# Squared-ReLU feed-forwards of a two-layer trunk as seven block products for eight, with operand sums passed through DRAM

## The chip, the cores and the metric

The kernel runs on one core of one Trainium2 chip, so there is no traffic between cores. The metric is the device time of one execution in microseconds (us), the median over runs. The profile is that of one execution: spans, durations and the granted TensorE clock are from it.

## The reference

All numbers are float32, with 1024 tokens of 1024 features. There are two layers: the first mixes tokens with a short gated convolution, the second with latent attention of eight heads. Each mixer is followed by a feed-forward of 4096 hidden features, and each of these four sub-layers by a normalisation over the residual:

```python
def _sq_relu_mlp(x, w1, w2):
    return jnp.square(jax.nn.relu(x @ w1)) @ w2
...
    for i in range(DEPTH):
...
        x = _layer_norm(ALPHA * x + y, ln_mix_g[i], ln_mix_b[i])
        x = _layer_norm(ALPHA * x + _sq_relu_mlp(x, ff_w1[i], ff_w2[i]), ln_ff_g[i], ln_ff_b[i])
    return x
```

Here `y` is the mixer's output, `w1` is 1024x4096, `w2` 4096x1024.

## The kernel before

**Products in three matmuls.** TensorE computes in a rounded type (float32r). Each float32 operand is therefore cut by `split` into a high part, a cast on ScalarE (L78), and a low part, source minus high part on VectorE (L79). `mm3` (L94) adds three matmuls into one PSUM bank: high by high (L96), high by low (L97), low by high (L98). `piece` (L85) loads a weight block of 128x1024 in two halves on the queue of SyncE (L90, tile `raw`, two buffers) and splits it into a `w` tile (five buffers). Activations with both their parts lie in `act` tiles of 128x1024 (34 buffers), products in eight PSUM banks of 128x512 (`pB`).

**A feed-forward.** `ffn` (L224) walks the hidden features in 32 blocks of 128, `m`. Tokens lie in two halves of 512, and `st.xt[half]` holds the transposed input as eight pairs of parts, one for each 128 features. For a block and a half, `ff1` sums eight products (24 matmuls), and `ffn_act` (L216) applies Relu on ScalarE (L218) and squares on VectorE (L219), then splits the result. Four blocks make a chunk. For a chunk, `token_out` (L118) sums four products (12 matmuls) for each of eight token tiles and two column halves and adds the bank to the residual tile `xrs[t]` on VectorE (L128 in the first chunk, which also multiplies the residual by ALPHA, L130 in later ones). The up-projection of the next chunk is written between the down-projections of two chunks.

**Around it.** The last chunk of every sub-layer but the final one is `last_chunk` (L199): after a tile's last addition, `ln_z` (L153) normalises it in place (two statistics L142, an aggregate L144, a root on ScalarE L146, four small operations L147 to L150, the scaling L155). Transposes (`ln_T`, L157) of the first four tiles are written behind tiles 4 to 7; those of the last four come in the next sub-layer, where `st.pump` takes them from the list. The gain and bias of the transposed input are applied on ScalarE (L162); those of the residual are applied by GpSimd in the first part of the next feed-forward (`tail_affine`, L211, through L180 and L181, 32 operations in place in `xrs`). After the second feed-forward, the final loop adds the last chunk, normalises, applies gain and bias, and stores the output from L668.

The program is one list in the order in which it is written. Each engine takes its own instructions of it in order and waits where an operand or a buffer isn't there yet. The same holds for the queues of SyncE, ScalarE and GpSimd that issue transfers.

## Time and profile before

| | |
|---|---|
| time, median of 3 runs | 2269.17 us (2267.36 to 2269.52) |
| span of the profiled execution, first to last instruction | 2269.7 us |
| TensorE matmul / weight load, share of the span | 98% / 82% |
| VectorE, ScalarE, GpSimd | 50%, 29%, 8% |
| transfers | 123.61 MB, mean 54 GB/s |

The profiled execution's own time is its span; nothing else lies around it. The median of the runs is 0.5 us below it. Shares are those of busy time over the whole span, which has stages of different kinds: the two feed-forwards run from about 375 to 1090 us and from about 1550 to 2260 us.

### The profile page before, as it was taken

Reading aid. Unit: us, or ns where it says so; the run is one execution under the profiler, and the core shown is the slowest. Engines: PE = TensorE matmul, PEld = TensorE weight load, DVE = VectorE, ACT = ScalarE, POOL = GpSimd, SP = SyncE. Lnnn points to the kernel's source line nnn. Section 1 sums busy time; section 2 is a strip of 40 time slices with the busy share of each in tenths; the row PEclk is TensorE's granted clock in tenths of the full one; section 3 lists DMA queues with packets and bytes.
Section 4 is the critical chain, followed back from the end, with each engine's and each line's share of the span. In section 5 each row is a group of like instructions: output and inputs, shape, how many; then the busy total and the mean of one; then the engine's idle time right before and its main releaser. Section 6 shows DMA issues by size and latency. Waiting matters only on the chain.

```text
span 2269.7 us, 25964 instructions
## 1 busy us (share of the span) xinstructions
PE 2217.9 (98%) x10360; PEld 1852.0 (82%) x10360; DVE 1135.9 (50%) x2002; ACT 650.9 (29%) x1239; POOL 184.9 (8%) x215
## 2 busy tenths in 40 slices
PE   8999998999999999999999999998999999999998
PEld 7888887788888888888888888786888888888886
DVE  5433459533433433436467778879343333333337
ACT  4111214321321311312456565333221221221222
POOL 0000007100000000000000002317000000000004
PEclk9999999999999999999999999998999999999999
DMA  5211211110210210212200011211111110110111
GB/s 188 100 38 44 68 48 47 56 56 19 75 53 23 75 47 28 74 44 78 76 6 21 15 39 47 93 47 56 47 65 36 48 63 30 56 56 28 65 47 74
DMA packets 64248, 123.61 MB, mean 54 GB/s; under 512 B 7280, under 2 KB 10352, under 8 KB 64128
## 3 DMA queue, kind: packets, MB, share of 16 engines
q1 hardware_dynamic: 56592, 99.64, 13.4%
q0 software_dynamic: 5088, 17.87, 2.3%
q10 hardware_dynamic: 2448, 4.46, 0.6%
q8 instruction: 81, 1.33, 0.2%
q14 instruction: 39, 0.32, 0.0%
HBM read 113.55 MB, written 8.39 MB: 54 GB/s over the span
## 4 chain that ended last, share of the span: by engine, by line
PE 88%; DVE 7%; DMA 2%; ACT 1%; issue 1%; SPq 0%; DVEq 0%; POOL 0%; ACTq 0%
PE pB L97 28%; PE pB L96 28%; PE pB L98 28%; DVE act L79 2%; DVE w L79 1%; DVE tmp L219 1%; PE pB L558 1%; DMA raw<-in_w_o 1%; ACT tmp L429 1%; PE pA L526 0%; PE pA L527 0%; PE pA L528 0%; PE pA L529 0%; PE pA L530 0%; DVE stat L142 0%
## 5 line engine op out<-in xcount | busy, mean ns | idle before, releaser
L96 PE MATMUL pB<-act,w 128*128 128x512 f32 x1608 | 631.1, 393 | 15.5 <-ACT act L78 9.7
L97 PE MATMUL pB<-act,w 128*128 128x512 f32 x1608 | 629.9, 392 | 0.3 <-DVE act L79 0.2
L98 PE MATMUL pB<-act,w 128*128 128x512 f32 x1608 | 628.8, 391 | 0.0
L96 PE MATMUL pB<-w,act 128*128 128x512 f32 (+1 forms) x1504 | 563.2, 375 | 1.8 <-DVE act L128 0.7
L97 PE MATMUL pB<-w,act 128*128 128x512 f32 (+1 forms) x1504 | 562.2, 374 | 1.7 <-DVE w L79 1.7
L98 PE MATMUL pB<-w,act 128*128 128x512 f32 (+1 forms) x1504 | 561.0, 373 | 0.0
L78 ACT CAST w<-raw 128x512 fp32r<-128x512 f32 x366 | 213.6, 613 | 793.0 <-PE pB L98 647.3
L96 PEld LDWEIGHTS pB<-act,w 128*128 128x128 f32 x1608 | 304.3, 189 | 79.4 <-ACT act L78 10.9
L97 PEld LDWEIGHTS pB<-act,w 128*128 128x128 f32 x1608 | 304.1, 189 | 64.3 <-DVE act L79 1.8
L98 PEld LDWEIGHTS pB<-act,w 128*128 128x128 f32 x1608 | 304.0, 189 | 63.7
L130 DVE TENSOR_TENSOR act<-act,pB 128x512 f32<-128x512 f32 x256 | 175.4, 685 | 348.7 <-PE pB L98 347.2
L96 PEld LDWEIGHTS pB<-w,act 128*128 128x128 f32 x1504 | 283.0, 188 | 56.5 <-ACT w L78 3.8
L97 PEld LDWEIGHTS pB<-w,act 128*128 128x128 f32 x1504 | 283.1, 188 | 54.2 <-DVE w L79 4.1
L98 PEld LDWEIGHTS pB<-w,act 128*128 128x128 f32 x1504 | 283.1, 188 | 49.7
L79 DVE TENSOR_TENSOR w<-raw,w 128x512 fp32r<-128x512 f32 x366 | 246.9, 695 | 151.1 <-ACT w L78 150.1
L219 DVE TENSOR_TENSOR tmp<-tmp 128x512 f32<-128x512 f32 x128 | 109.2, 853 | 266.3 <-ACT tmp L218 266.2
L79 DVE TENSOR_TENSOR act<-tmp,act 128x512 fp32r<-128x512 f32 x204 | 160.1, 795 | 58.0 <-ACT act L78 58.0
L78 ACT CAST act<-tmp 128x512 fp32r<-128x512 f32 x204 | 123.6, 621 | 148.4 <-DVE tmp L219 77.3
L218 ACT ACTIVATE tmp<-pB 128x512 f32<-128x512 f32 x128 | 76.3, 596 | 284.4 <-PE pB L98 283.8
L128 DVE SCALAR_TENSOR_TENSOR act<-act,pB 128x512 f32<-128x512 f32 x64 | 43.8, 686 | 92.2 <-PE pB L98 92.0
L667 POOL TENSOR_TENSOR act<-act,row 128x512 f32<-128x512 f32 x13 | 17.2, 1320 | 651.5 <-DVE act L666 651.0
L180 POOL TENSOR_TENSOR act<-act,row 128x512 f32<-128x512 f32 x40 | 61.9, 1565 | 92.2 <-DVE stat L142 69.4
(112 smaller groups left out, 1252.9 us busy)
## 6 DMA issues: line engine op xcount, KB each, us to landing
raw<-in_w_f SPq DMA_DIRECT2D x256, 256.0 KB, 2.7
raw<-in_w_sci SPq DMA_DIRECT2D x42, 256.0 KB, 2.7
act<-in_xT ACTq DMA_DIRECT2D x16, 256.0 KB, 4.4
act<-in_x POOLq DMA_DIRECT2D x8, 512.0 KB, 9.4
raw<-in_w_sco SPq DMA_DIRECT2D x16, 256.0 KB, 2.7
row<-in_grow POOLq DMA_DIRECT2D x16, 256.0 KB, 3.7
spill<-act POOLq DMA_DIRECT2D x8, 512.0 KB, 2.9
raw<-in_w_o SPq DMA_DIRECT2D x16, 256.0 KB, 2.7
```

The source lines that it names most:

```text
L78: nc.scalar.copy(hi, src)
L79: nc.vector.tensor_tensor(lo, src, hi.bitcast(F32), op=ALU.subtract)
L96: nc.tensor.matmul(ps, lh, rh, start=first, stop=False)
L97: nc.tensor.matmul(ps, lh, rl, start=False, stop=False)
L98: nc.tensor.matmul(ps, ll, rh, start=False, stop=last)
L128: nc.vector.scalar_tensor_tensor(xr[:, s], xr[:, s], ALPHA, ps, op0=ALU.mult, op1=ALU.add)
L130: nc.vector.tensor_tensor(xr[:, s], xr[:, s], ps, op=ALU.add)
L180: engs[d].tensor_tensor(xr[:, s], xr[:, s], gr[d], op=ALU.mult)
L218: nc.scalar.activation(r, ps, AF.Relu)
L219: nc.vector.tensor_tensor(r, r, r, op=ALU.mult)
L429: nc.scalar.copy(b[j * 32:(j + 1) * 32], ps[k * 32:(k + 1) * 32])
L558: nc.tensor.transpose(ps[:, j * P:(j + 1) * P], p[:, (q4 + j) * P:(q4 + j + 1) * P], ident)
```

## The change

Both projections of both feed-forwards are cut in 2x2 blocks and computed with seven products of blocks and their sums (Winograd's form of Strassen's algorithm) in place of eight products.

**Up-projection.** The hidden blocks are taken in 16 pairs `p` and `p + 16`, the features in two halves of four, the tokens in two halves. A product `k` of a pair is four `mm3`, 12 matmuls, in one bank. `load` brings the two weight blocks of a pair; `sums` makes four sums of weight blocks on GpSimd (L255 to L258); `operand` splits the weight operand of one product into an `fp` tile (eight buffers), and `ahead` keeps six operands ready. The inputs of products 4 to 7 are differences of the transposed input, made once in `combine` (L346, for `k == 7` on GpSimd, else on VectorE). `begin` and `rest` add the banks into the four output blocks on VectorE (`add`, L293), apply Relu and Square on ScalarE, make four sums, and store seven operands for the down-projection in DRAM (`hs`) through SyncE. The first four pairs (`LEAD`) run products 1 and 2, then 3, then 6, 7, 5 and 4; transposes of the last four token tiles lie between them, and the four `combine` calls between the products 3.

**Down-projection.** It runs product by product, in the order 1, 2, 5, 6, 3, 7, 4, each over all 16 pairs in four banks, 192 matmuls. `second` loads the hidden operand from `hs` and a quarter of a weight block, both through SyncE, makes a sum on GpSimd for products 5, 6, 7 and 4, and splits both; `ahead2` keeps four ready, or more while eight `fp` tiles last. After each product VectorE adds the four banks to the halves of the residual tiles that take it (`parts`; L435 after the first, L437 later). The residual is no longer kept in SBUF over the up-projection: `last_chunk` stores the normalised tiles in DRAM (`zs`), and during product 1 `residual` loads them through SyncE and GpSimd applies gain and bias (L195, L196). After products 3 and 4, `finish` normalises four tiles each: `keep_z` in the first layer, `emit`, which also applies the last gain and bias and stores the output, in the second.

SBUF tiles `w`, `raw`, `tmp`, `row`, `half` (19 buffers) and `fp` now come from a pool for each stage (`stage_pool`). The attention, the convolution and their tiles are otherwise as they were; `spill` is written tile by tile in `keep_z` and no longer at the start of the attention.

```diff
+    def stage_pool(name):
+        pool = tc.tile_pool(name=name, bufs=1, reuse_waits="tile")
+        work.append(pool.__enter__())
+        return pool
...
+    def hbt():
+        return work[-1].tile([P, HB], F32, tag="half", bufs=19, name="half")
+    def fpair():
+        t = work[-1].tile([P, 2 * HB], F32R, tag="fp", bufs=8, name="fp")
+        return t[:, 0:HB], t[:, HB:2 * HB]
...
+            nc.gpsimd.dma_start(zs[t * P:(t + 1) * P], xrs[t])
...
-        st.add_T(l, 1, xrs)
+        st.add_T(l, 1, xrs, (4, 5, 6, 7, 0, 1, 2, 3))
...
-    def tail_affine(l, xrs):
-        gr = ln_rows(l)
-        for t in range(NT):
-            ln_affine(xrs[t], gr, (nc.gpsimd, nc.gpsimd))
...
+    NPAIR = NF // 2
+    LEAD = 4
+    AHEAD = 6
+    AHEAD2 = 4
+    def ffn(l, lnl, st, zs, hs, out_l, finish):
...
+        def load(p):
+            raw[p] = [act1(F32), act1(F32)]
+            for i in range(2):
+                nc.sync.dma_start(raw[p][i], w_f1[l, p + NPAIR * i])
+        def sums(p):
+            (a11, a12), (a21, a22) = [(r[:, 0:HB], r[:, HB:T]) for r in raw[p]]
+            s1 = s1w[p] = hbt()
+            nc.gpsimd.tensor_tensor(s1, a21, a22, op=ALU.add)
+            nc.gpsimd.tensor_tensor(a21, a11, a21, op=ALU.subtract)
+            nc.gpsimd.tensor_tensor(a11, s1, a11, op=ALU.subtract)
+            nc.gpsimd.tensor_tensor(a12, a12, a11, op=ALU.subtract)
+        def operand(p, k):
+            r1, r2 = raw[p]
+            src = {1: r1[:, 0:HB], 2: r1[:, HB:T], 3: r1[:, HB:T], 4: r2[:, HB:T], 5: s1w.get(p),
+                   6: r1[:, 0:HB], 7: r2[:, 0:HB]}[k]
+            wh, wl = fpair()
+            split(src, wh, wl)
+            return wh, wl
+        seq = [(p, k) for p in range(LEAD) for k in (1, 2)] + [(p, 3) for p in range(LEAD)]
+        seq += [(p, k) for p in range(LEAD) for k in (6, 7, 5, 4)]
+        seq += [(p, k) for p in range(LEAD, NPAIR) for k in (1, 2, 6, 7, 5, 3, 4)]
+        ready = {}
+        def ahead(n):
+            while seq and len(ready) < n:
+                p, k = seq.pop(0)
+                if p not in raw:
+                    load(p)
+                if k == (3 if p < LEAD else 6):
+                    sums(p)
+                ready[p, k] = operand(p, k)
+            if not seq and len(ready) < 4:
+                ahead2(4 - len(ready))
+        def product(p, k):
+            ahead(AHEAD)
+            wp = ready.pop((p, k))
...
+            for j in range(4):
+                mm3(ps, cols(wp, j * P, (j + 1) * P), xc[k][j], j == 0, j == 3)
+            return ps
...
+        def begin(p):
+            s1 = hbt()
+            nc.scalar.copy(s1, product(p, 1))
+            c11 = hbt()
+            add(c11, s1, product(p, 2))
+            held[p] = [s1, c11, None]
+        def rest(p):
+            s1, c11, c12 = held.pop(p)
+            ps = product(p, 6)
+            if c12 is None:
+                u2 = s1
+                add(u2, s1, ps)
+                u3 = hbt()
+                add(u3, u2, product(p, 7))
+                ps = product(p, 5)
+                add(u2, u2, ps)
+                c22 = hbt()
+                add(c22, u3, ps)
+                add(u2, u2, product(p, 3))
...
+            a11, a21, a12, a22 = c11, c12, c21, c22
+            for a in (a11, a21, a22, a12):
+                nc.scalar.activation(a, a, AF.Relu)
+                nc.scalar.activation(a, a, AF.Square)
+            s1 = hbt()
+            add(s1, a21, a22)
+            s2 = hbt()
+            add(s2, s1, a11, ALU.subtract)
+            s3 = a21
+            add(s3, a11, a21, ALU.subtract)
+            s4 = hbt()
+            add(s4, a12, s2, ALU.subtract)
+            for k, a in ((1, a11), (4, a22), (5, s1), (6, s2), (7, s3), (2, a12), (3, s4)):
+                nc.sync.dma_start(hs[k, p], a)
+        def combine(j):
+            b11, b12 = st.y[j][:, 0:HB], st.y[j][:, HB:T]
+            b21, b22 = st.y[j + 4][:, 0:HB], st.y[j + 4][:, HB:T]
+            for k, o, a, b in ((5, b11, b12, b11), (7, b12, b22, b12), (6, b22, b22, b11), (4, b21, b22, b21)):
+                (nc.gpsimd if k == 7 else nc.vector).tensor_tensor(o, a, b, op=ALU.subtract)
+                h, lo = act()
+                split(o, h, lo)
+                xc.setdefault(k, []).append((h, lo))
+        for p in range(LEAD):
+            load(p)
+        for p in range(LEAD):
+            begin(p)
+            st.pump(2)
+        st.pump(len(st.todo))
+        xc[3] = st.xt[1][4:8]
+        for p in range(LEAD):
+            held[p][2] = hbt()
+            add(held[p][2], held[p][0], product(p, 3))
+            combine(p)
+        order2 = (1, 2, 5, 6, 3, 7, 4)
+        seq2 = [(k, p) for k in order2 for p in range(NPAIR)]
...
+        def second(k, p):
+            hr = hbt()
+            nc.sync.dma_start(hr, hs[k, p])
+            hh, hl = act()
+            split(hr, hh, hl)
+            r, c = {1: (0, 0), 2: (1, 0), 5: (0, 1), 6: (1, 1), 3: (1, 1), 7: (0, 1), 4: (1, 0)}[k]
+            w = part(ta, p) if k == 1 else part(tb, p) if k == 3 else hbt()
+            nc.sync.dma_start(w, w_f2[l, p + NPAIR * r, :, c * HB:(c + 1) * HB])
+            if k in (5, 6, 4):
+                t = part(ta, p)
+                i = (w, t) if k != 4 else (t, w)
+                nc.gpsimd.tensor_tensor(t, *i, op=ALU.subtract)
+                w = t
+            elif k == 7:
+                t = part(tb, p)
+                nc.gpsimd.tensor_tensor(t, t, w, op=ALU.subtract)
+                w = t
+            wp = fpair()
+            split(w, *wp)
+            return hh, hl, wp
...
+        def residual(t, gr):
+            xr = xrt()
+            nc.sync.dma_start(xr, zs[t * P:(t + 1) * P])
+            ln_affine(xr, gr, (nc.gpsimd, nc.gpsimd))
+            xrs.append(xr)
+        parts = {1: ((0, 0), (0, 1), (1, 0), (1, 1)), 2: ((0, 0),), 5: ((0, 1), (1, 1)),
+                 6: ((0, 1), (1, 0), (1, 1)), 3: ((0, 1),), 7: ((1, 0), (1, 1)), 4: ((1, 0),)}
+        for k in order2:
+            pss = [psB() for _ in range(4)]
+            for p in range(NPAIR):
+                ahead2(AHEAD2)
+                hh, hl, wp = ready2.pop((k, p))
+                for j in range(4):
+                    c = slice(j * P, (j + 1) * P)
+                    mm3(pss[j], (hh[:, c], hl[:, c]), wp, p == 0, p == NPAIR - 1)
+                if k == 1 and p >= 4:
+                    if p == 4:
+                        gr = ln_rows(lnl, hbt)
+                    if p < 4 + NT:
+                        residual(p - 4, gr)
+                if k in (7, 4) and p >= 3:
+                    st2.pump(1)
+            ahead2(AHEAD2)
+            for j in range(4):
+                for i, d in parts[k]:
+                    o = xrs[4 * i + j][:, d * HB:(d + 1) * HB]
+                    if k == 1:
+                        nc.vector.scalar_tensor_tensor(o, o, ALPHA, pss[j], op0=ALU.mult, op1=ALU.add)
+                    else:
+                        nc.vector.tensor_tensor(o, o, pss[j], op=ALU.subtract if k == 4 else ALU.add)
+                if k in (3, 4):
+                    finish(4 * (k == 4) + j, xrs)
+            if k in (3, 4) and out_l is not None:
+                st2.add_T(out_l, int(k == 4), xrs)
...
+        ln_z(xrs[t])
+        nc.gpsimd.dma_start(spill[t * P:(t + 1) * P], xrs[t])
+    st, xrs = ffn(0, 0, st, zs[0], hs, 1, keep_z)
...
+    ffn(1, 2, st, zs[1], hs, None, emit)
```

**Order on GpSimd at the start of the first feed-forward.** Before, the queue holds the loads of the gain and bias rows (`row`) and then the 32 operations on the residual tiles (`act_364` to `act_371`):

```order
L173 DMA row_2721<-in_grow 128x512
L180 TENSOR_TENSOR act_364<-act_364,row_2715 128x512
L180 TENSOR_TENSOR act_365<-act_365,row_2715 128x512
L181 TENSOR_TENSOR act_364<-act_364,row_2719 128x512
L181 TENSOR_TENSOR act_365<-act_365,row_2719 128x512
```

In the changed kernel the same place holds weight sums of four pairs (the last of the four sets stands here; `act_2617` and `act_2618` are the raw weight blocks of pair 3) and behind them the differences of the inputs for product 7:

```order
L255 TENSOR_TENSOR half_2808<-act_2618 128x512
L256 TENSOR_TENSOR act_2618<-act_2617,act_2618 128x512
L257 TENSOR_TENSOR act_2617<-half_2808,act_2617 128x512
L258 TENSOR_TENSOR act_2617<-act_2617 128x512
L346 TENSOR_TENSOR act_2403<-act_2482,act_2403 128x512
L346 TENSOR_TENSOR act_2413<-act_2492,act_2413 128x512
L346 TENSOR_TENSOR act_2423<-act_2502,act_2423 128x512
L346 TENSOR_TENSOR act_2433<-act_2512,act_2433 128x512
```

The residual's operations have gone to the down-projection, and the four differences stand behind all 16 sums of the leading pairs.

**Order on VectorE after the first down-product.** There is no such place before, since each bank was added as soon as it was full. Now the row is this (`pB_5242` to `pB_5245` are the four banks, `act_5361` and so on the residual tiles, `fp` and the `act` rows of L86 the low parts of the next operands):

```order
L86 TENSOR_TENSOR fp_5632<-half_5630,fp_5632 128x512
L435 SCALAR_TENSOR_TENSOR act_5361<-act_5361,pB_5242 128x512
L86 TENSOR_TENSOR act_5649<-half_5647,act_5649 128x512
L86 TENSOR_TENSOR fp_5654<-half_5652,fp_5654 128x512
L435 SCALAR_TENSOR_TENSOR act_5471<-act_5471,pB_5242 128x512 x2
L435 SCALAR_TENSOR_TENSOR act_5389<-act_5389,pB_5243 128x512 x2
L435 SCALAR_TENSOR_TENSOR act_5499<-act_5499,pB_5243 128x512 x2
L435 SCALAR_TENSOR_TENSOR act_5416<-act_5416,pB_5244 128x512 x2
L435 SCALAR_TENSOR_TENSOR act_5526<-act_5526,pB_5244 128x512 x2
L435 SCALAR_TENSOR_TENSOR act_5444<-act_5444,pB_5245 128x512 x2
L435 SCALAR_TENSOR_TENSOR act_5554<-act_5554,pB_5245 128x512 x2
L86 TENSOR_TENSOR act_5691<-half_5689,act_5691 128x512
```

Sixteen additions that wait for residual tiles stand in the row, 14 of them in one piece, ahead of the split for the operand that follows.

**Order on VectorE at the end of the first layer.** Before, the split of the attention's first weight (`w_7116`) stands ahead of the last chunk's additions (L130) and normalisations:

```order
L219 TENSOR_TENSOR tmp_6681<-tmp_6681 128x512
L79 TENSOR_TENSOR w_7116<-raw_7117,w_7116 128x512
L79 TENSOR_TENSOR w_7116<-raw_7121,w_7116 128x512
L79 TENSOR_TENSOR act_6684<-tmp_6681,act_6684 128x512
L130 TENSOR_TENSOR act_364<-act_364,pB_6723 128x512
L142 BN_STATS stat_6751<-act_364 128x6
```

Now the same weight is `w_8037`, and the piece ahead of it is the last addition and the normalisations of tiles 5 to 7 (`act_5499`, `act_5526`, `act_5554`):

```order
L437 TENSOR_TENSOR act_5554<-act_5554,pB_7660 128x512
L164 TENSOR_SCALAR stat_7998<-stat_7998 128x1
L161 RECIPROCAL stat_8010<-stat_8010 128x1
L156 BN_STATS stat_8022<-act_5554 128x6
L169 TENSOR_SCALAR act_5499<-act_5499,stat_7998 128x1024
L162 TENSOR_SCALAR stat_8010<-stat_8010 128x1
L156 BN_STATS stat_8022<-act_5554 128x6
L163 TENSOR_SCALAR stat_8010<-stat_8010 128x1
L158 BN_AGGR stat_8022<-stat_8022 128x2
L86 TENSOR_TENSOR w_8037<-raw_8038,w_8037 128x512
```

The weight's split has moved behind additions that wait for the last matmuls of the layer, and behind most of the four normalisations.

## Rows read from the trace of the kernel before

**Rows 1.** Page: busy times, and the chain that ended last.

```profile
PE 2217.9 (98%) x10360; PEld 1852.0 (82%) x10360; DVE 1135.9 (50%) x2002; ACT 650.9 (29%) x1239; POOL 184.9 (8%) x215
...
PE 88%; DVE 7%; DMA 2%; ACT 1%; issue 1%; SPq 0%; DVEq 0%; POOL 0%; ACTq 0%
```

**Rows 2.** Busy time by stretch: columns PE, PEld, DVE, ACT, POOL, clock, DMA, GB/s.

```profile
900.00:1000.00 100.00, 100.00 (x443) 82.81 (x442) 34.98 (x53) 18.37 (x32) 0.00 (x0) 1.00 0.13 43
```

**Rows 3.** Groups of instructions by line: count | busy us, mean ns | idle before.

```profile
L98 PE MATMUL pB<-w,act 128*128 128x512 f32 x1280 | 497.6, 389 | 0.0
...
L79 DVE TENSOR_TENSOR w<-raw,w 128x512 fp32r<-128x512 f32 x354 | 242.7, 706 | 151.1 <-ACT w L78 150.1
...
L130 DVE TENSOR_TENSOR act<-act,pB 128x512 f32<-128x512 f32 x256 | 175.4, 685 | 348.7 <-PE pB L98 347.2
...
L218 ACT ACTIVATE tmp<-pB 128x512 f32<-128x512 f32 x128 | 76.3, 596 | 284.4 <-PE pB L98 283.8
```

**Rows 4.** VectorE in order of time: start, us, line, pieces.

```profile
352.76 0.67 DVE L130 TENSOR_TENSOR act<-act,pB 128x512 f32<-128x512 f32 x1
...
369.24 1.27 DVE L79 TENSOR_TENSOR w<-raw,w 128x512 fp32r<-128x512 f32 x2
...
371.14 0.69 DVE L142 BATCH_NORM_STATS2 stat<-act 128x6 f32<-128x512 f32 x1
371.87 0.21 DVE L144 BATCH_NORM_AGGREGATE stat<-stat 128x2 f32<-128x12 f32 x1
372.44 0.16 DVE L147 RECIPROCAL stat<-stat 128x1 f32<-128x1 f32 x1 [0.36 <-ACT stat L146]
...
374.24 0.81 DVE L155 TENSOR_SCALAR act<-act,stat 128x1024 f32<-128x1024 f32 x1
...
383.29 3.47 DVE L79 TENSOR_TENSOR act<-tmp,act 128x512 fp32r<-128x512 f32 x2
...
391.79 11.11 DVE L219 TENSOR_TENSOR tmp<-tmp 128x512 f32<-128x512 f32 x1
```

**Rows 5.** GpSimd in order of time.

```profile
384.47 3.44 POOL L180 TENSOR_TENSOR act<-act,row 128x512 f32<-128x512 f32 x2
...
397.38 2.53 POOL L180 TENSOR_TENSOR act<-act,row 128x512 f32<-128x512 f32 x2
```

**Rows 6.** TensorE at the start of the first feed-forward.

```profile
375.10 3.04 PE L160 MATMUL pB<-ident,act 128*128 128x128 f32 x13 [6.01 <-DVE act L155]
...
384.03 1.91 PE L160 MATMUL pB<-ident,act 128*128 128x128 f32 x16
...
399.19 0.39 PE L98 MATMUL pB<-act,w 128*128 128x512 f32 x1
404.13 0.80 PE L96 MATMUL pB<-act,w 128*128 128x512 f32 x1 [4.55 <-ACT act L78]
```

**Rows 7.** Busy time by stretch, at the starts of both feed-forwards.

```profile
300.00:400.00 100.00, 92.36 (x430) 76.86 (x428) 81.09 (x116) 28.67 (x53) 47.56 (x34) 0.97 0.14 45
400.00:500.00 100.00, 95.86 (x410) 78.77 (x411) 43.94 (x64) 27.60 (x49) 3.41 (x4) 0.97 0.18 57
405.00:410.00 5.00, 5.00 (x12) 3.94 (x13) 3.32 (x6) 3.57 (x7) 0.00 (x0) 0.51 0.04 16
...
1500.00:1600.00 100.00, 88.70 (x397) 72.64 (x396) 87.34 (x124) 38.29 (x69) 50.41 (x36) 0.93 0.16 51
```

**Rows 8.** DMA: one early stretch, and one load of the queue of SyncE.

```profile
5.00:10.00 5.00, 4.13 (x10) 3.28 (x11) 3.37 (x8) 3.49 (x9) 0.00 (x0) 1.00 0.93 273
...
raw<-in_w_f SPq DMA_DIRECT2D x256, 256.0 KB, 2.7
...
700.44 1.26 SPq L90 DMA_DIRECT2D raw<-in_w_f  x2
```

**Rows 9.** The end of the program.

```profile
2259.35 0.39 PE L98 MATMUL pB<-w,act 128*128 128x512 f32 x1
...
2265.67 0.35 ACTq L668 DMA_DIRECT2D out<-act  x1
```

More of the change, by code (lines that the diff above doesn't have):

```diff
@@ L59, in tmp @@
     def tmp(w=T):
-        return sb.tile([P, w], F32, tag="tmp", bufs=4, name="tmp")
+        return work[-1].tile([P, w], F32, tag="tmp", bufs=4, name="tmp")
     def row(w=HB):
-        return sb.tile([P, w], F32, tag="row", bufs=4, name="row")
+        return work[-1].tile([P, w], F32, tag="row", bufs=4, name="row")
     def stat(w=8):
@@ L190, in pump, with add_T, last_chunk @@
                 self.todo.pop(0)()
[L192 removed]
+        def add_T(self, l, half, xrs, order=range(NK)):
             def mk(k):
                 def f():
[L195 to L200 removed]
+                    if self.keep:
+                        if self.y[k] is None:
+                            self.y[k] = act1(F32)
+                        y = self.y[k][:, half * HB:(half + 1) * HB]
+                    else:
+                        y = act1(F32)[:, 0:HB]
+                    self.xt[half][k] = ln_T(l, half, k, xrs, y, not (self.keep and half and k < 4))
+                return f
+            self.todo += [mk(k) for k in order]
+    def last_chunk(l, lhs_of, wps, xrs, first, zs):
+        st = Stage(True)
         for t in range(NT):
@@ L265, in trunk_kernel @@
     scope = psum("p0")
     banks.append(scope.__enter__())
+    stage = stage_pool("s0")
+    zs = [dr.tile([T, D], F32, name="z%d" % i) for i in range(2)]
+    hs = {(k, p): dr.tile([P, HB], F32, name="h%d_%d" % (k, p)) for k in range(1, 8) for p in range(NPAIR)}
     xt0 = [[None] * NK, [None] * NK]
@@ L648, in trunk_kernel, with emit @@
     wo = [piece(w_o[4 + i]) for i in range(4)]
-    st = last_chunk(2, lambda t: [ot[4 + i, t // 4] for i in range(4)], wo, xrs, False)
-    lhs_of, w2 = ffn(1, st, xrs, after=lambda: tail_affine(2, xrs))
-    gr = ln_rows(3)
-    for t in range(NT):
+    st = last_chunk(2, lambda t: [ot[4 + i, t // 4] for i in range(4)], wo, xrs, False, zs[1])
+    stage.__exit__(None, None, None)
+    stage = stage_pool("s3")
+    ogr = []
+    def emit(t, xrs):
+        if not ogr:
+            ogr.extend(ln_rows(3, hbt))
+        gr = ogr
         xr = xrs[t]
-        token_out(t, lhs_of(t), w2, xr, False)
         mu, r, s = ln_stats(xr)
```

111 lines of the change are left out of this document (53 added, 58 removed).

## The prediction, made before the changed kernel ran

> **What bounds the kernel now.** Read the page first. TensorE is busy for 98% of the span and holds 88% of the chain that ended last; VectorE has 7% of it, transfers 2% [rows 1]. The table by stretch then tells whether that busy engine is at its pace: in the middle of a feed-forward it is busy for 100.00 of 100 us with 443 matmuls at a granted clock of 1.00, while VectorE works 35 us, ScalarE 18 us and the DMA engines 0.13 [rows 2]. The reader is to see a stage in which nothing but the number of matmuls counts. One matmul of 128x512 is worth 100/443 = 0.2257 us there (the 389 ns of the group [rows 3] overlap, so they are not the price). Twelve of them, one product step of the changed kernel, are worth 2.71 us.
>
> The only idle TensorE near the change is at the start of each feed-forward: 7.64 + 4.14 = 11.8 us in the two stretches around the first one [rows 7]. The two waits are a transpose that waits 6.0 us for the normalisation on VectorE and a matmul that waits 4.6 us for a split on ScalarE, itself behind a VectorE operation that took 11.1 us [rows 4, 6]. After the second wait the clock was 0.51 (1.00 is the 2.4 GHz level, 0.51 near the 1.2 GHz one), and 12 matmuls took 5 us instead of 2.7 [rows 7]: 2.3 us more.
>
> **What VectorE pays beside GpSimd.** This decides the costs, since the change gives GpSimd sums of both projections. Two splits (an add with both inputs in SBUF) alone take 1.27 us, so 0.6 us each in a row [rows 4]. Beside GpSimd two take 3.47 us, and GpSimd's own two 3.44 us, against 2.53 us alone [rows 4, 5]. So a pair of one VectorE and one GpSimd operation takes 1.72 us, and a GpSimd operation costs VectorE up to 1.72 - 0.6 = 1.12 us. An add with one input in PSUM took 0.67 us in the middle of such a run [rows 4]: those are free of it.
>
> **The change part by part.**
>
> *A. Matmuls removed.* Seven of eight: 4 x 192 = 768 fewer over two layers with two projections each. 768 x 0.2257 = -173.4 us. The weight loads go with them one to one.
>
> *Steady up-projection.* Per pair of feature blocks TensorE has 7 x 2.71 = 19.0 us. VectorE has 7 splits, 7 adds from PSUM and 4 sums in SBUF, 18 x 0.6 = 10.8 us, and beside it 4 GpSimd sums: 10.8 + 4 x 1.12 = 15.3 us. ScalarE has 7 casts, 8 Relu or Square and a copy, 16 x 0.6 = 9.6 us [rows 3]. SyncE issues 9 transfers at 0.63 us, 5.7 us, and they move 2.75 MB, 145 GB/s; the trace shows 273 GB/s at a DMA share of 0.93 [rows 8], so a full rate of about 290. All of it lies under TensorE: nothing. Without that cover the VectorE time would be the price.
>
> *Steady down-projection.* A product step needs two loads of 256 KB (193 GB/s), two casts, two splits. Where a weight sum is made (four of seven products) VectorE needs 0.6 + 1.72 + 0.45 for the adds from PSUM and the normalisations spread over these steps = 2.77 us against 2.71 us; in the other steps some 1.6 us. Six to eight operands are held ahead, so the excess of 4 us over 64 steps is swallowed: nothing.
>
> The Trainium skill, page "SBUF — State Buffer", section "Who interferes with whom", says that a VectorE instruction with two SBUF inputs and a GpSimd instruction that reads SBUF exclude each other for the whole instruction, and it speaks against sums on GpSimd. The trace agrees in kind, and in size the pair took 1.72 us, not 0.6 + 1.27 = 1.87; by the rule these steps would cost VectorE 2.92 us and the result would be the third rival's. The 11.1 us of one operation show that more than one GpSimd operation can go first.
>
> *B. Start of a feed-forward.* GpSimd makes 16 sums for the first four pairs and only then the first difference of the inputs: 17 x 1.72 = 29 us, from about 2 us after the last matmul of the stage before. VectorE, with its own splits in between, is no earlier. Behind that wait stand 39 VectorE operations up to the last input operand, 39 x 0.6, and three more GpSimd operations, 3 x 1.12: 27 us. So the sixteenth product ends at about 2 + 29 + 27 + 1.5 = 59.5 us, where TensorE has 16 x 2.71 + 32 transposes (16 go in 1.9 us [rows 6]) = 47.2 us of work. The loss is 12.3 us, with the slow clock 15. Now it is 11.8 + 2.3 = 14; the second feed-forward's start has 11.3 us idle and a clock of 0.93 [rows 7], much the same. So +1 each, +2 in all; from -10 each (GpSimd runs at 1.27 us and VectorE is not late) to +12 each.
>
> *C. Up to down.* SyncE sends the last sums out before it loads the fourth operand. The chain is add, Relu, Square, sum, 2.4 us, then about ten transfers of 256 KB, 9.6 us at 273 GB/s, cast and split 1.2 us: 13.2 us against the four steps that are ready, 10.9. +2 each, +4; from 0 to 10.
>
> *D. After the first down-product.* The affine of the residual (32 GpSimd operations), before in the start of the stage, now runs beside the 16 steps of the first product. Its first load is issued behind about eleven transfers and lands some 14 us into the product. From there 24 pairs of VectorE and GpSimd operations take 41 us, and eight more GpSimd operations 10: the last tile is ready 65 us into the stage. TensorE is done with the product at 45.4 us and has four operands ready, so it runs dry at 56.3. VectorE stands in the row of 16 adds at the last tile, with the next split behind it: 65 + 1.2 + 1.2 = 67.4. Stall 11 us, with the slow clock 13; +26 in all. If GpSimd were not late, the adds and seven splits, 23 x 0.6 = 13.8, would still outlast 10.9: at least 3 each. At most 20.
>
> *E. After the fifth product.* Four normalisations stand in VectorE's order. One is an add, two statistics, an aggregate, the wait for the root, four small ones and the scaling: 0.6 + 1.2 + 0.2 + 0.2 + 0.8 + 0.8 [rows 4] = 3.8 us without the wait, which the others fill. 15 us, 7 splits 4 us, less 2 us by which the first tile ends earlier: 17 to 21 us against five ready operands, 13.6. +5, with the clock +7 in the first layer; nothing in the second, where seven are ready (19 us). From 0 to 15.
>
> *F. End of the first layer.* The first attention weight's split stands behind three of these normalisations, 12.5 us, less the 2: 10 us of idle TensorE, with the clock 12, where there was none. From 6 to 18.
>
> *G. End of the program.* Now 2269.7 - 2259.7 = 10 us lie behind the last matmul [rows 9], with one tile left to finish. After the change four tiles are left: 4 x 3.8 us, nine affine operations of 0.7 to 1.3 us on VectorE, some waits for ScalarE, and a transfer of 2 us: 22 us. +12; from 8 to 18.
>
> Sum: -173.4 + 2 + 4 + 26 + 7 + 12 + 12 = -110. The profiled span is 2269.7 us, 0.5 us over the median of the runs, so no correction is due: 2159 us.
>
> **The rivals.**
> 1. *The stalls are hidden.* If GpSimd runs ahead at 1.27 us and the operands held cover the rows of adds, B to E sum to about -10 and F and G to 14: 2269.7 - 173.4 + 4 = 2100, with one of the waits left 2110. For it: the low VectorE share [rows 2]. Against: the alternating runs [rows 4, 5].
> 2. *Transfers pace the down-projection.* A step of 512 KB at 180 GB/s takes 2.91 us, +0.2 x 224 = 45 us, and the first product with its residual (12.6 MB) 70 us instead of 45, for which 11 of D's stall is already counted: +20 or so. 2225 us. For: the loads wait in one queue behind the stores. Against: 273 GB/s in the trace. The Trainium skill, page "HBM Reference", section "Specifications (TRN2)", gives about 358 GB/s per core; by that this rival falls and C and D shrink. No run here shows that rate.
> 3. *The lock lasts for the whole GpSimd operation.* VectorE then needs 2.92 us in 128 steps, +27 us less what the ready operands absorb, and D grows by 4 each: 2190 us. For it: the row of 11.1 us, the rule above. Against: 1.72, not 1.87.
> 4. *Slower.* In the down-projection both splits of a step meet a GpSimd operation: 2 x 1.72 + 0.45 = 3.89 us, +1.18 x 128 = 151 us: 2310 us. It decides from 3.58 us per such step, where (2269.7 - 2159) / 128 = 0.87 us are lost in each. For: every split took 1.72 us while GpSimd had work. Against: GpSimd has only one operation per step.
>
> **How the numbers follow.** Chances: forecast 0.62, rival 1 0.08, rival 2 0.12, rival 3 0.10, rival 4 0.08. The low bounds of B to G together give 2095 and the high ones 2225, but they will not all meet; 2115 to 2220 leaves out rival 4, about half of rivals 1 and 2 and the corners, some 0.2. Within 0.2% (4.5 us, about what a measurement of this kernel can tell) of 2269 lies almost nothing: 0.01. Faster 0.91, slower 0.08.
>
> **What would show it.** Right: 9562 matrix instructions for 10330; stretches in the middle of either projection again at 443 matmuls per 100 us and clock 1.00; TensorE gaps of 8 to 15 us after the first down-product, before the attention and about 40 us into each feed-forward, each with a clock near 0.5 behind it; some 22 us behind the last matmul. Wrong: fewer than 440 matmuls in steady stretches with VectorE near 100% (rivals 3, 4) or the DMA share near 1 (rival 2); no gap after the first product (D).

## The result, and the profile after

The changed kernel takes 2170.43 us (median of 4 runs, 2168.10 to 2172.85), the kernel before 2269.35 us beside it: a ratio of 0.9563, with a 95% interval of 0.9549 to 0.9576. The forecast was 2159 us in a range of 2115 to 2220. By the profiled executions' spans it went from 2269.7 to 2170.9 us, 98.8 us less, where the forecast had 110.

The page's busy times and the table by stretch answer to [rows 1, 2, 7] (columns as there):

```profile
PE 2063.0 (95%) x9592; PEld 1709.2 (79%) x9592; DVE 1498.6 (69%) x2426; ACT 942.4 (43%) x1711; POOL 618.3 (28%) x495
```

```profile
400.00:500.00 100.00, 89.51 (x379) 72.39 (x378) 84.43 (x127) 56.38 (x97) 22.86 (x17) 0.93 0.46 159
500.00:600.00 100.00, 100.00 (x443) 82.89 (x442) 63.80 (x93) 51.30 (x85) 31.27 (x24) 1.00 0.44 155
...
700.00:710.00 10.00, 9.30 (x41) 7.71 (x42) 6.95 (x8) 4.92 (x9) 6.45 (x5) 1.00 1.04 400
...
740.00:750.00 10.00, 8.79 (x37) 6.27 (x35) 10.00 (x13) 0.00 (x0) 10.00 (x8) 1.00 0.00 0
750.00:760.00 10.00, 3.68 (x9) 2.92 (x10) 9.27 (x16) 3.52 (x6) 4.34 (x4) 0.66 0.62 183
...
810.00:820.00 10.00, 7.78 (x32) 5.79 (x33) 10.00 (x13) 4.24 (x7) 5.41 (x4) 1.00 0.72 211
```

The stretch from 500 to 600 us lies in the up-projection: 443 matmuls at a clock of 1.00, as before the change. TensorE does 768 matmuls less at the same pace, which is the whole gain. The other lines are places where part of it is given back. These are the longest of TensorE's waits, in order of time; the numbers in brackets are the idle time before the matmul and what ended it. The second layer's start waits like the first's, 6.14 us at 1535.61 us:

```profile
413.78 1.22 PE L110 MATMUL pB<-act,fp 128*128 128x512 f32 x2 [6.14 <-ACT act L85]
...
700.70 1.20 PE L110 MATMUL pB<-fp,act 128*128 128x512 f32 x4 [1.31 <-ACT fp L85]
...
756.32 0.80 PE L111 MATMUL pB<-fp,act 128*128 128x512 f32 x1 [6.79 <-DVE fp L86]
...
1018.41 0.50 PE L110 MATMUL pB<-act,w 128*128 128x512 f32 x1 [3.00 <-ACT w L85]
...
1878.85 0.79 PE L111 MATMUL pB<-fp,act 128*128 128x512 f32 x1 [7.97 <-DVE fp L86]
...
2091.97 0.79 PE L110 MATMUL pB<-fp,act 128*128 128x512 f32 x1 [5.59 <-ACT fp L85]
...
2102.97 0.51 PE L111 MATMUL pB<-fp,act 128*128 128x512 f32 x1 [2.09 <-DVE fp L86]
...
2146.21 0.39 PE L112 MATMUL pB<-fp,act 128*128 128x512 f32 x1
```

The group of line L112 gives the ends of the four feed-forward stages: count, shortest, median and longest duration in ns, first and last start. `pB<-act,fp` is the up-projection, `pB<-fp,act` the down-projection.

```profile
L112 PE MATMUL pB<-act,fp x448: 388/390/629, 363.9 to 686.7; 128*128 128x512 f32 x150
L112 PE MATMUL pB<-fp,act x448: 388/390/629, 687.4 to 1015.0; 128*128 128x512 f32 x150
...
L112 PE MATMUL pB<-act,fp x448: 387/390/629, 1485.6 to 1809.1; 128*128 128x512 f32 x150
L112 PE MATMUL pB<-fp,act x448: 387/390/629, 1809.8 to 2146.2; 128*128 128x512 f32 x150
```

1344 matmuls at 0.2257 us are 303.3 us. The stages last 323.9, 328.3, 325.3 and 337.1 us from the first matmul of one to the first of the next. Less 3.3 us of transposes in the first three, they lose 17.2, 21.6, 18.6 and 33.7 us. In the trace of before, the two feed-forwards lasted 720.8 and 717.3 us against 693.4 us of matmuls and 6.7 and 3.3 us of transposes: they lost 20.7 and 20.5 us, nearly all of it at their starts. So the up-projections give back nothing new (35.8 us now, 41.2 before) and the down-projections 55.3 us. The attention between them lasts 468.8 us against 459.8, and behind the last matmul lie 24.5 us instead of 10.1.

### The profile page after: what moved, and what is told of

Read it like the earlier page. It is cut to its first block, busy times and chain, and to the rows that moved or that the text cites. A ratio compares the mean times of both kernels' runs of the same rounds, so it can differ in the third digit from the quotient of the medians.

```text
span 2170.9 us, 27353 instructions
## 1 busy us (share of the span) xinstructions
PE 2063.0 (95%) x9592; PEld 1709.2 (79%) x9592; DVE 1498.6 (69%) x2426; ACT 942.4 (43%) x1711; POOL 618.3 (28%) x495
## 5 line engine op out<-in xcount | busy, mean ns | idle before, releaser
L86 DVE TENSOR_TENSOR fp<-act,fp 128x512 fp32r<-128x512 f32 x384 | 338.9, 889 | 105.7 <-ACT fp L85 104.0
L111 PE MATMUL pB<-fp,act 128*128 128x512 f32 x896 | 355.1, 396 | 26.4 <-DVE fp L86 26.3
L85 ACT CAST fp<-act 128x512 fp32r<-128x512 f32 x384 | 235.8, 620 | 321.7 <-PE pB L112 220.2
L110 PE MATMUL pB<-act,fp 128*128 128x512 f32 x896 | 352.0, 394 | 15.2 <-ACT act L85 14.5
L110 PE MATMUL pB<-fp,act 128*128 128x512 f32 x896 | 350.1, 393 | 10.7 <-ACT fp L85 7.8
L111 PE MATMUL pB<-act,fp 128*128 128x512 f32 x896 | 352.0, 393 | 6.5 <-DVE act L86 6.5
L112 PE MATMUL pB<-act,fp 128*128 128x512 f32 x896 | 351.7, 393 | 2.0 <-DVE fp L86 2.0
L112 PE MATMUL pB<-fp,act 128*128 128x512 f32 x896 | 352.0, 393 | 0.0
L293 DVE TENSOR_TENSOR half<-half,pB 128x512 f32<-128x512 f32 x232 | 155.3, 684 | 148.5 <-PE pB L112 147.9
L110 PE MATMUL pB<-act,w 128*128 128x512 f32 x584 | 230.6, 395 | 9.4 <-ACT w L85 9.3
L86 DVE TENSOR_TENSOR act<-half,act 128x512 fp32r<-128x512 f32 x224 | 226.1, 1027 | 13.1 <-ACT act L85 12.9
L112 PE MATMUL pB<-act,w 128*128 128x512 f32 x584 | 229.9, 394 | 0.5 <-DVE w L86 0.5
L111 PE MATMUL pB<-act,w 128*128 128x512 f32 x584 | 230.0, 394 | 0.2 <-DVE act L86 0.2
L111 PEld LDWEIGHTS pB<-fp,act 128*128 128x128 f32 x896 | 170.1, 190 | 71.0 <-DVE fp L86 36.4
L110 PEld LDWEIGHTS pB<-act,fp 128*128 128x128 f32 x896 | 169.4, 189 | 53.0 <-ACT act L85 17.4
L110 PEld LDWEIGHTS pB<-fp,act 128*128 128x128 f32 x896 | 169.2, 189 | 47.9 <-ACT fp L85 9.1
L111 PEld LDWEIGHTS pB<-act,fp 128*128 128x128 f32 x896 | 169.8, 189 | 43.1 <-DVE act L86 8.0
L112 PEld LDWEIGHTS pB<-act,fp 128*128 128x128 f32 x896 | 169.7, 189 | 38.3 <-DVE fp L86 3.2
L112 PEld LDWEIGHTS pB<-fp,act 128*128 128x128 f32 x896 | 170.0, 190 | 35.1
L85 ACT CAST act<-half 128x512 fp32r<-128x512 f32 x224 | 136.8, 619 | 108.5 <-DMA half<-h 78.6
L110 PE MATMUL pB<-w,act 128*128 128x512 f32 (+1 forms) x480 | 165.1, 345 | 3.0 <-ACT w L85 1.8
L111 PE MATMUL pB<-w,act 128*128 128x512 f32 (+1 forms) x480 | 163.6, 342 | 1.3 <-DVE w L86 1.3
```

The lines of the kernel that those rows point to most:

```text
L85: nc.scalar.copy(hi, src)
L86: nc.vector.tensor_tensor(lo, src, hi.bitcast(F32), op=ALU.subtract)
L110: nc.tensor.matmul(ps, lh, rh, start=first, stop=False)
L111: nc.tensor.matmul(ps, lh, rl, start=False, stop=False)
L112: nc.tensor.matmul(ps, ll, rh, start=False, stop=last)
L293: nc.vector.tensor_tensor(o, a, b, op=op)
```

## Experiments

All are changes of the changed kernel; ratios are to the kernel before, with the 95% interval. 2170.4 us is the time to compare with.

**All sums on VectorE.**

```diff
-            nc.gpsimd.tensor_tensor(s1, a21, a22, op=ALU.add)
+            nc.vector.tensor_tensor(s1, a21, a22, op=ALU.add)
...
-                (nc.gpsimd if k == 7 else nc.vector).tensor_tensor(o, a, b, op=ALU.subtract)
+                nc.vector.tensor_tensor(o, a, b, op=ALU.subtract)
...
-                nc.gpsimd.tensor_tensor(t, *i, op=ALU.subtract)
+                nc.vector.tensor_tensor(t, *i, op=ALU.subtract)
```

> All weight sums of both projections and the input differences of product 7 go from GpSimd to VectorE; the affine of the residual stays on GpSimd. Theory (a GpSimd operation costs VectorE up to 1.12 us, the same operation on VectorE costs it 0.6 us, and the start of a feed-forward waits for sixteen sums in a row on GpSimd): the waits of TensorE around 398 to 414 us and 1520 to 1536 us (11.9 us each in the changed kernel) shrink to under 6 us each, the small waits after the second down-product (2 to 3 us each) go away, steady stretches stay at 443 matmuls per 100 us; 2145 to 2158 us. The wait of 7 to 8 us after the first down-product stays. Rival (VectorE is near its bound in the projections, and each operation taken from GpSimd lengthens its row): steady stretches fall below 440 matmuls per 100 us with VectorE near 100%, 2175 us or more.

It took 2128.97 us, 0.9375 (0.9356 to 0.9393): 41 us less, where 12 to 25 were expected. In its table by stretch the start has no wait left:

```profile
400.00:500.00 100.00, 100.00 (x442) 82.57 (x441) 87.98 (x145) 53.89 (x95) 0.00 (x0) 1.00 0.48 167
500.00:600.00 100.00, 100.00 (x443) 82.81 (x442) 73.37 (x118) 49.54 (x86) 0.00 (x0) 1.00 0.45 161
```

The starts gave 15 and 16 us, and the waits near 2092 and 2103 us went as well, which I had not expected here. The small waits after the second product are gone, as expected. The wait after the first product stayed, at 8.0 us in both layers, and the first layer's down-projection got 4 us longer, with transposes that wait 1.6 and 2.3 us near 921 us. VectorE's share in the steady stretch rose from 63.8 to 73.4 us in 100 and cost nothing. The rival falls.

**Only the up-projection's sums on VectorE** (the first two edits above, without the third).

> Only the up-projection's weight sums and the input differences of product 7 go to VectorE; the down-projection's sums stay on GpSimd. Theory (the start of a feed-forward waits for sixteen sums in a row on GpSimd, and the late wait in the second feed-forward for GpSimd's weight sums behind its operations on the output): both starts gain as in the run with all sums moved, 15 and 17 us, the waits of TensorE near 2092 and 2103 us (of the changed kernel) stay; 2136 to 2142 us. Rival (the starts gained from the lower load of GpSimd later on, or the late wait is SyncE's): either the starts keep 5 us or more of their waits, or the late wait goes as well and the time is 2125 to 2132 us.

2139.74 us, 0.9429 (0.9415 to 0.9443), as the theory had it. The starts have no wait left but 0.7 us at their first matmul, and the late waits of the second layer are there, 5.6 and 2.7 us. So of the 41 us the starts carry about 31, and the down-projection's sums the other 11.

**Affine of the residual on VectorE.**

```diff
-            ln_affine(xr, gr, (nc.gpsimd, nc.gpsimd))
+            ln_affine(xr, gr, (nc.vector, nc.vector))
```

> Only the gain and bias of the residual during the first down-product go from GpSimd to VectorE, 32 operations of 0.6 us. Theory (the wait after the first down-product is for VectorE's row of sixteen additions, which stands behind the last residual tile that GpSimd is late with): VectorE needs 16 x 2 x 0.6 + 32 x 0.6 = 38 us in a product of 43 us without GpSimd beside it, the residual tiles are ready when the product ends, and of the 6.8 and 8.0 us of wait about 0 to 3 us each are left; with the clock behind them and the smaller waits inside the product, 2150 to 2158 us. Rival A (the loads that wait for the buffers of the gain and bias rows, or the DMA engines at a share of 1.04, are what is late): the waits stay, 2168 to 2173 us. Rival B (VectorE gets too much work): the wait moves into the first product, 2168 us or more.

2154.35 us, 0.9487 (0.9473 to 0.9501). The wait after the first down-product, in TensorE's order of time:

```profile
750.58 0.50 PE L111 MATMUL pB<-fp,act 128*128 128x512 f32 x1 [2.59 <-DVE fp L86]
```

The 6.8 us became 2.6, the 8.0 of the second layer likewise 2.6. GpSimd's lateness cost 16 us in all; I take the rest to be the row of additions itself.

**Gain and bias rows in buffers of their own.** In the changed kernel SyncE's queue stands for 21 us in this stage, since its next load gets a buffer in which a gain row lies until GpSimd's last tile:

```profile
729.09 0.32 SPq L375 DMA_DIRECT2D half<-h  x1
750.69 0.33 SPq L380 DMA_DIRECT2D half<-in_w_f  x1
```

```diff
-                        gr = ln_rows(lnl, hbt)
+                        gr = ln_rows(lnl, lambda: act1(F32)[:, 0:HB])
```

> The changed kernel with the gain and bias rows of the residual in four activation tiles instead of four of the buffers through which the loads of the down-projection go round; GpSimd keeps the affine. Theory (the wait after the first product is for VectorE's row of additions, which GpSimd's affine holds up): SyncE's queue no longer stands from 729 to 751 us, but the waits of 6.8 and 8.0 us stay within 1 us; 2166 to 2173 us. Rival (the loads behind those buffers were late): the waits shrink to 3 us or less; 2150 to 2160 us.

2169.94 us, 0.9561 (0.9547 to 0.9575). The loads went on until 745 us, and the wait stayed:

```profile
756.59 0.80 PE L111 MATMUL pB<-fp,act 128*128 128x512 f32 x1 [6.87 <-DVE fp L86]
```

In the second layer it grew from 8.0 to 9.3 us, a little more than the 1 us that I allowed, and did not shrink. So a queue that visibly stands for 21 us was not the cause.

**Output stores on another queue.**

```diff
-            (nc.scalar if t == NT - 1 and d == 0 else nc.sync).dma_start(out
+            (nc.gpsimd if t < 4 else nc.scalar if t == NT - 1 and d == 0 else nc.sync).dma_start(out
```

> The stores of the first four finished output tiles (eight DMAs) are issued by GpSimd's queue instead of SyncE's. Theory (in the second feed-forward the loads of the last two down-products stand in SyncE's queue behind output stores, which wait for GpSimd's last operation on a tile): the waits of TensorE of 5.6 and 2.1 us near 2092 and 2103 us go away with the slow clock behind them, -8 to -11 us, 2159 to 2163 us; the first layer is unchanged. Rival (GpSimd itself is late: its weight sums stand behind the operations on the output tiles): the waits stay within 2 us, 2168 to 2173 us.

2174.19 us, 0.9578 (0.9564 to 0.9592): my theory falls. The late wait is one piece now, and longer:

```profile
2092.37 0.79 PE L111 MATMUL pB<-fp,act 128*128 128x512 f32 x1 [10.05 <-DVE fp L86]
```

The wait at 2092 us lies in the sixth product, 168 of its 192 matmuls in. That product's own sums (L388) were all done by 2042.7 us, so they are not what is late. TensorE waits for a weight cast on ScalarE (5.59 us in the list above, `fp` L85), and ScalarE's order of time in the changed kernel says why:

```profile
2074.52 0.62 ACT L85 CAST act<-half 128x512 fp32r<-128x512 f32 x1 [10.65 <-DMA out<-act]
...
2090.26 1.14 ACT L85 CAST act<-half 128x512 fp32r<-128x512 f32 x2 [5.28 <-DMA out<-act]
2091.31 0.61 ACT L85 CAST fp<-act 128x512 fp32r<-128x512 f32 x1
```

The casts of hidden operands for the last product write `act` tiles, and they wait until output stores have emptied such tiles; the weight casts stand behind them in ScalarE's order. The stores wait for GpSimd's operations on the output (L859, L860), and those stand behind weight sums of the last product (L384), which wait for loads, and further on between them:

```profile
2067.35 1.29 POOL L384 TENSOR_TENSOR act<-act,half 128x512 f32<-128x512 f32 x1 [2.82 <-DMA half<-in_w_f]
2068.60 1.28 POOL L859 TENSOR_TENSOR act<-act,half 128x512 f32<-128x512 f32 x1
...
2081.20 1.74 POOL L384 TENSOR_TENSOR act<-act,half 128x512 f32<-128x512 f32 x1
2082.90 1.74 POOL L859 TENSOR_TENSOR act<-act,half 128x512 f32<-128x512 f32 x1
2084.61 3.40 POOL L860 TENSOR_TENSOR act<-act,half 128x512 f32<-128x512 f32 x2
2087.97 1.70 POOL L384 TENSOR_TENSOR act<-act,half 128x512 f32<-128x512 f32 x1
```

Another queue for the stores changes nothing in this: ScalarE's longest such wait in this run is 13.04 us, again for `out<-act`. With the sums on VectorE the wait was gone although the stores were still in SyncE's queue, and with only the up-projection's sums moved it stayed. So GpSimd's order is the cause, but by way of the finished output tiles, which are late, and not of the sums that TensorE needs next.

**The last product bank by bank.**

```diff
+                if k in (4,) and p >= NPAIR - 4:
+                    continue
...
+            ops = [(p, ready2.pop((k, p))) for p in range(NPAIR - 4, NPAIR) if k in (4,)]
             ahead2(AHEAD2)
             for j in range(4):
+                for p, (hh, hl, wp) in ops:
+                    c = slice(j * P, (j + 1) * P)
+                    mm3(pss[j], (hh[:, c], hl[:, c]), wp, False, p == NPAIR - 1)
```

> In the last down-product the last four pairs are run bank by bank, so that the four banks end 2.7 us apart and not together. Theory (24.5 us behind the last matmul and the waits of 5.4 us before the attention are four normalisations, 3.8 us each, in one row on VectorE): three of the four move under TensorE's work; behind the last matmul about 24.5 - 3 x 2.7 to 24.5 - 3 x 3.8 = 13 to 17 us are left, and the attention's start loses 2 to 5 us less; 2155 to 2162 us. Rival (the end is the time from the last tile's normalisation over GpSimd, ScalarE and the store alone, whatever stands before it): 22 us or more stay behind the last matmul, 2168 us or more.

2159.24 us, 0.9511 (0.9496 to 0.9525). The gain of 11 us is 8 at the end and 4 in the attention, which lasts 464.6 us instead of 468.8. The span is 2158.6 us, and the last matmul ends 17 us before its end:

```profile
2141.60 0.39 PE L112 MATMUL pB<-fp,act 128*128 128x512 f32 x1
```

**Hidden operands loaded twice.**

```diff
             nc.sync.dma_start(hr, hs[k, p])
+            nc.sync.dma_start(hbt(), hs[k, p])
```

> The changed kernel with each hidden operand of the down-projection loaded a second time into a buffer that nothing reads, 768 KB a step instead of 512. Theory (transfers are not what paces the down-projection; the trace of the changed kernel shows 396 to 400 GB/s at a DMA share of 1.04): a step's loads take 1.97 us of 2.71, only the start of the down-projection and the first product with its residual (16.8 MB, 42 us of 45) get later; 5 to 20 us more, 2175 to 2190 us. Rival (the 273 GB/s at 0.93 seen before are near the rate that such loads get): a step takes 2.7 us or more in loads, the first product 58 us instead of 45; 2200 us or more.

2169.95 us, 0.9561 (0.9547 to 0.9576), where 5 to 20 us more were expected. It is not longer in all, but not for one reason. The start got worse, with a wait of 4.1 us in one piece in both layers, and the first layer's down-projection is 8 us longer (transposes also wait 3.4 us near 942 us). The small waits after the second product are gone, and in the second layer the wait near 2092 us did not come up. The trace suggests why: the loads come later, so the last product's sums no longer stand ahead of GpSimd's work on the output, which starts 9 us earlier than in the changed kernel, though the sixth product starts 7 us later:

```profile
2059.83 1.29 POOL L860 TENSOR_TENSOR act<-act,half 128x512 f32<-128x512 f32 x1 [1.45 <-ACT act L859]
```

In between, from 1950 to 2080 us, both kernels issue 575 matmuls, at 186 GB/s in the changed kernel and 283 here. Transfers do not pace these steps.

**Together.** All sums and the affine on VectorE, and the last product bank by bank; and the same with `AHEAD2 = 7`.

> All weight sums, the input differences and the affine of the residual on VectorE, and the last four pairs of the last down-product bank by bank: three of the runs before in one. Theory (their gains lie in different places and add): 2129 - 16 - 11 = 2102 us, 2096 to 2110 us; after the first down-product a wait of 2 to 3 us is left, at the end 13 to 17 us. Rival (VectorE, which then carries all of it, becomes the bound in a down-product): steady stretches of the down-projection fall under 440 matmuls per 100 us, 2115 us or more.

> The same, with seven operands of the down-projection kept ready instead of four. Theory (the waits left after the first and the fifth product are rows of additions and normalisations on VectorE, longer than the four steps that are ready): seven steps are 19 us against 14 to 17 us, the waits of 2 to 4 us there go; 5 to 12 us under the run with four, 2090 to 2098 us. Rival (the operands are not there sooner, since loads and splits run at the same pace whatever is written ahead): the same time within 3 us.

2101.80 us, 0.9261 (0.9246 to 0.9277), where the sum of the three gains gave 2102; and 2095.78 us, 0.9235 (0.9221 to 0.9249). With seven operands the wait after the first product is gone in both layers.

**The attention's first weight.** In that last kernel the wait ahead of the attention is 5 us, and SyncE issues the weight's load only here, when the last matmul has run:

```profile
991.75 6.78 SPq L104 DMA_DIRECT2D raw<-in_w_lat  x4
...
996.11 1.20 ACT L85 CAST w<-raw 128x512 fp32r<-128x512 f32 x2 [1.61 <-DMA raw<-in_w_lat]
996.76 0.69 DVE L86 TENSOR_TENSOR w<-raw,w 128x512 fp32r<-128x512 f32 x1 [1.79 <-ACT w L85]
996.78 0.80 PE L110 MATMUL pB<-act,w 128*128 128x512 f32 x1 [5.06 <-ACT w L85]
```

```diff
+                if k == 4 and p == NPAIR - 5 and pre is not None:
+                    pre()
...
+    def pre():
+        wh, wl = act1(), act1()
+        for a in (0, HB):
+            r = hbt()
+            nc.sync.dma_start(r, w_lat[0][:, a:a + HB])
+            split(r, wh[:, a:a + HB], wl[:, a:a + HB])
+        early.append((wh, wl))
...
-    lw = [piece(w_lat[i]) for i in range(3)]
+    lw = early + [piece(w_lat[i]) for i in range(1, 3)]
```

> The run with seven operands ready, and the attention's first weight loaded and split into activation tiles during the last down-product of the first layer. Theory (the 5.1 us before the attention are that weight's load, which SyncE issues only when the last matmul has given back the memory of the stage, and its split): the wait goes with the slow clock behind it, 6 to 8 us under that run, 2087 to 2091 us. Rival (the wait is for VectorE's row of additions and normalisations, and the first transposes of the last four tiles take its place): 2 us or less, 2093 to 2097 us.

2090.02 us, 0.9204 (0.9189 to 0.9220), 5.8 us less: the wait went, and one of 2.1 us for the transposes of the last tiles came in its place. Both theories have a part in it.

**Transposes later** (in addition, `p >= 7` for `p >= 3` at `st2.pump`).

> The run before, and the transposes of the first four tiles written from the eighth pair of the sixth down-product on instead of the fourth. Theory (the waits of 2.7 and 1.6 us near 909 us are transposes that stand in TensorE's order before VectorE has normalised their tiles): they go, 3 to 5 us less, 2083 to 2087 us. Rival (VectorE's row of normalisations makes the operands late as well): the wait moves to a matmul, less than 2 us gained.

2082.89 us, 0.9174 (0.9160 to 0.9188). It is 7 us less, more than expected. The down-projection of the first layer now has no wait behind its start (2.6 us before 683 us), from its table by stretch:

```profile
690.00:990.00 300.00, 300.00 (x1341) 248.35 (x1340) 245.48 (x431) 133.93 (x234) 5.92 (x11) 1.00 0.61 207
```

## Why the prediction was right, and what its terms missed

**A** held: 443 matmuls per 100 us in steady stretches, so -173.4 us. Against the spans, the rest has to be +74.6: B gave -5.4 (forecast +2), the down-projections +55.3 (C, D and E: +37), F +9.0 (+12), G +14.4 (+12), and 1.3 us lie in the stage before the first feed-forward.

**B**, mechanism right, size wrong. The waits of a start sum to 11.9 us (the last of them, 6.1 us, is shown above; the waits of before are in [rows 6]), and to 11.8 before. With the slow clock and the matmuls that come late a start loses 17 and 19 us, where I had 15, and it lost 20 to 21 before, where I had 14. The sixteen sums ran from 369.5 to 394.3 us, 1.55 us each where I took 1.72, and in the two runs with these sums on VectorE 2 to 3 us of a start's loss were left. They take away the row on GpSimd and what its operations cost VectorE together, so how the loss divides between the two is not shown. I had not seen that ScalarE's cast for product 3 waits for a whole set of sums too, and holds back everything behind it:

```profile
394.31 1.67 ACT L85 CAST fp<-act 128x512 fp32r<-128x512 f32 x3 [3.85 <-POOL act L258]
```

**C** was right in size: 2.4 and 2.7 us of waits, forecast 2 each. Some 1 us of matmuls that come late follows.

**D**, the largest term, held in place and cause, and nearly in size. VectorE and GpSimd around the wait:

```profile
745.71 7.25 DVE L435 SCALAR_TENSOR_TENSOR act<-act,pB 128x512 f32<-128x512 f32 x12
753.15 0.69 DVE L435 SCALAR_TENSOR_TENSOR act<-act,pB 128x512 f32<-128x512 f32 x1 [0.19 <-POOL act L196]
754.37 0.69 DVE L435 SCALAR_TENSOR_TENSOR act<-act,pB 128x512 f32<-128x512 f32 x1 [0.54 <-POOL act L196]
754.98 0.68 DVE L86 TENSOR_TENSOR act<-half,act 128x512 fp32r<-128x512 f32 x1
755.58 0.69 DVE L86 TENSOR_TENSOR fp<-half,fp 128x512 fp32r<-128x512 f32 x1
```

The last addition waits for GpSimd (L196), 67 us into the stage (forecast 65), and the split that TensorE needs stands behind it. The idle time was 6.8 and 8.0 us instead of 11, since TensorE reached the place later: ahead of it lie small waits of some 2 us in the first layer and 1 in the second, with VectorE at 10.00 of 10 us. With these and the slow clock behind the wait, the second product takes 53.9 and 55.4 us where 192 matmuls are worth 43.3: 10.6 and 12.1 us lost, 13 each forecast. "At least 3 each", if GpSimd were on time, measured 2.6 each.

**E** was wrong in size: I counted 17 to 21 us for a row of normalisations, and it took 12, with the first split after 8:

```profile
922.99 1.28 DVE L437 TENSOR_TENSOR act<-act,pB 128x512 f32<-128x512 f32 x2
...
930.71 0.82 DVE L86 TENSOR_TENSOR fp<-act,fp 128x512 fp32r<-128x512 f32 x1
...
934.64 0.81 DVE L169 TENSOR_SCALAR act<-act,stat 128x1024 f32<-128x1024 f32 x1
```

The first splits stand inside the row, and the row ended 5 us under its bound: no wait in the first layer, where I had 7 us.

**F** is near in size, 9 for 12 us (5.4 us of waits, where I had 10, then matmuls at a granted clock of 0.50, the 1.2 GHz level, from 1020 to 1026 us), but only in part right in its cause: ahead of VectorE's row stands the load, which SyncE issues at 1015.4 us, with the last matmul of the stage.

**G** was +14 for +12, and the run bank by bank showed that it is the row of four tiles.

**What no term had** came to 21 us in two places; the error is only 11 us because B and E came out some 7 us each under their terms. That the forecast lies so near is in part luck.

The first place is the third product, which loses 4.0 us in the first layer and 4.3 in the second. In steady steps with a weight sum I priced 2.77 us and called the excess swallowed. But the loads come early, and then GpSimd makes sums without a pause:

```profile
770.02 29.94 POOL L384 TENSOR_TENSOR act<-half,act 128x512 f32<-128x512 f32 x18 [15.68 <-DMA half<-in_w_f]
```

```profile
778.32 5.18 DVE L86 TENSOR_TENSOR act<-half,act 128x512 fp32r<-128x512 f32 x3
```

Eighteen sums in 30 us, 1.66 us each, and beside them every split takes 1.7 us, both of a step. That is the condition of the fourth rival, for 36 us and not for the whole stage; the price is 2.6 us of waits after the second product (the stretch 810 to 820 above) and what follows them. In the run with all sums on VectorE the third product loses nothing. The second place is the late wait of the second layer, "nothing in the second, where seven are ready": seven were not ready, since ScalarE's casts waited for the stores of output tiles, which GpSimd finished late. The sixth and seventh products of the second layer lose 12.5 us together, and its down-projection 12 us more than that of the first.

The rivals: the first (stalls hidden) fell by the waits above; a TensorE nearly without waits in the projections is seen only in the last kernel here, at 2083 us, and not by the way that rival had, since there the sums are VectorE's. The second (transfers) fell: 400 GB/s in the changed kernel's trace, and the run with double loads. The third and the fourth hold only where GpSimd has a run of work. The Trainium skill, page "SBUF — State Buffer", section "Who interferes with whom", says that a VectorE instruction with two SBUF inputs and a GpSimd instruction that reads SBUF lock each other out; the pair of 1.7 us agrees in kind. What I overlooked is that a sum moved to VectorE costs it 0.6 us and no pair at all.

Three remarks on the numbers. The prediction's "9562 matrix instructions for 10330" should read 9592 for 10360 [rows 1], which the trace shows; the difference of 768 is right. A pair's transfers in the up-projection are 2.88 MB and not 2.75, so 152 GB/s, and the trace shows 155. TensorE's waits in one piece were 6 to 8 us and, before the attention, 3.0, not the gaps of 8 to 15 that were to show the forecast right.

The spans of all later runs lie 1.7 to 2.0 us under the same executions' device time, so something does lie around the span. It takes no part in the error: the change is 98.8 us by the spans and 98.9 by the medians.

## What to carry to other kernels

When TensorE paces a stage, matmuls saved are worth their full pace; what decides the rest are the seams, where a row of work on another engine is longer than the operands held ready. Price a helper engine by its order, not by its share: GpSimd was busy for 28% of the span, and 57 us (41 and 16 in the two runs that moved its work to VectorE) hung on the places where it stood. A queue that stands still is a cause only if what is behind it is needed first; give it a buffer of its own and look.

## What the hardware showed that was not expected

- The DMA engines moved 400 GB/s at a share of 1.04 in the changed kernel, where [rows 8] gave 273 at 0.93 and I took 290 for the full rate. That is above the 358 GB/s which the prediction cited. The Trainium skill, page "Perfetto Trace Analysis", section "Roofline", says that a core which runs alone can pull more than that share, up to about 435 GB/s over its 16 DMA engines; the measurement agrees with this.
- VectorE's small operations on 128x1 are listed with 0.2 us each. Where those of two tiles alternate, some start 0.12 us apart (926.77 and 926.89 us); those of one tile in a row start 0.25 us apart (1025.15, 1025.39 and 1025.64 us). In the row after the fifth product the tiles alternate, and four normalisations with their additions took 12 us, not 15 and more.
- In the steady up-projection GpSimd's sums cost VectorE little: 93 operations in 63.8 us with them, 118 in 73.4 us without, 0.69 against 0.62 us each, so about 6 us for 24 sums. The price of 1.12 us that I took for each holds where the engines' rows lie side by side.
